# Two-layer decoder trunk: fixed order of the inner norms, two PSUM banks for the turned chunks, and a fourth kept-back unit outside the weight slots

## The chip, the core and the metric

The kernel runs on one core of a Trainium2 chip. The metric is device microseconds (us) of one execution, smaller is better. Engines are called by the profile's names: PE (TensorE, matmuls), PEld (its weight loads), DVE (VectorE), ACT (ScalarE), POOL (GpSimd) and SP (SyncE, which issues the transfers here).

## The reference, cut to what matters

Two layers over 256 tokens of width 2048. Each layer has a token mixer (layer 0 forgetting attention, "fox"; layer 1 sliding-window attention, "swa") and a gated ConvFFN. Each of these four sub-layers ends in a LayerNorm, and the next begins with a modulation by columns that come from the conditioning vector `c`:

```python
for i in range(DEPTH):
    sh1, sc1, g1, sh2, sc2, g2 = split(silu(c) @ ada_w[i] + ada_b[i], 6)
    h = x * (1 + sc1) + sh1
    y = fox_attention(h, ...) if i % 2 == 0 else swa_attention(h, ...)
    x = layer_norm(ALPHA * x + (1 + g1) * y, ln_mix_g[i], ln_mix_b[i])
    h = x * (1 + sc2) + sh2
    y = conv_ffn(h, ...)
    x = layer_norm(ALPHA * x + (1 + g2) * y, ln_ffn_g[i], ln_ffn_b[i])
```

## The kernel before, in words

**Arithmetic.** Every large product is done in split form: an operand is rounded to a "high" part (fp32r) and the rest is a "low" part, and three matmuls (high x high, high x low, low x high) are summed. Weights stream in blocks: a *unit* is two 128-row slices of the weight by 512 columns. `stream` loads it (`w`), ACT rounds it to the high part (`wh`, L252), DVE subtracts to get the low part (`wl`, L263). `wh` and `wl` come from a pool of four slots each; the raw `w` tiles come from a pool of six, which the rows of the conditioning matrix (`wa`, L395) and the LayerNorm gains (`ln`, L667) share.

**Activations.** `x` holds the 256 tokens as two halves of 128 rows each, the *first rows* (t = 0) and the *second rows* (t = 1), by four column blocks of 512 (d = 0 to 3). `hH`/`hL` is the turned (transposed), modulated input of a sub-layer, in 16 chunks of 128 columns; both lie in one tile, so the profile and the order call both `hH`.

**The joints.** Between two sub-layers the last column block of the last projection must be finished, added to `x` and normalised before the next projection can start. Three such inner *joints* exist, near 450, 1188 and 1452 us; class `Edge` writes them. To overlap, the last projection keeps its last four units back (`x_mm_end`): for these it does the first rows at once and the second rows afterwards, while the first rows go through residual, statistics and norm. The next projection's first block does the reverse (`x_mm_start`): its first four units are done for the first rows, then for the second rows. The kept units need storage beyond the four slots: `spares` puts three of them into free parts of the `hH` buffer, the fourth stays in a weight slot.

`residual_rows` is the chain of one half: product times gate (L634), add to `x` (L636), statistics (L638, L641, L643), reciprocal root on POOL (L644), the negated mean times root (L646). `normalise(d, ts, act)` scales a column block on ACT (L659) for the halves in `act`, else on DVE (L661). `turn_rows` transposes four chunks of one half on PE (L514) into one PSUM bank; `mod_rows` then makes for a pair of chunks the high parts on ACT (L522) and an fp32 copy `t` on DVE (L526) or ACT (L524), and DVE subtracts to the low part (L527). The chunks from 8 on are turned for both halves together (`mod_turn` L477, `mod_pair` L491, L495, L84, L85).

**What sets the order.** Each engine runs its own list in order. A scheduler lays out the lists at build time; an instruction under `pin` keeps its place in program order, the others may be moved. `affine` (L680, L681) multiplies the normalised `x` by the LayerNorm gains later, in the background, one instruction pair per step of the stream.

## Time and profile before

| | |
|---|---|
| median of 3 runs | 2201.17 us (2200.56 to 2203.99) |
| profiled execution | 2202.95 us, its span 2201.1 us |
| granted PE clock, mean | 0.991 |
| PE / DVE / ACT busy | 2135.2 / 1767.4 / 1175.3 us of the span |
| HBM read | 594.18 MB, 271 GB/s over the span |

A row of the groups reads: line, engine, operation, output <- inputs, shapes, count, then busy us and mean ns of one, then idle time ahead of it and what ended that. A row of the timeline reads: start, duration, engine, line, operation; in brackets the idle time before it and the engine and tile that ended it. A row of the stages gives for each engine busy us and (in brackets) instructions, then the granted PE clock, the DMA share and GB/s.

### The profile page before, as it was taken

What the parts mean: (1) busy time and instruction counts of PE and PEld (TensorE: products, weight loads), DVE (VectorE), ACT (ScalarE), POOL (GpSimd) and SP (SyncE); (2) the same over time, 40 slices, a digit from 0 to 9 for tenths busy, and PEclk for the clock granted to TensorE, in tenths of its full rate; (3) what the DMA queues carried; (4) which work ended last, traced back from release to release, by engine and by line L of the source; (5) the groups of instructions that cost most, each with busy time, mean ns of one, the idle gap of its engine ahead of it and who ended that gap; (6) DMA issues with size and microseconds to landing.
All of it is one profiled execution on the core that took longest, in us unless ns stands there. A gap on an engine that the chain in (4) does not pass through costs nothing.

```text
span 2201.1 us, 35820 instructions
## 1 busy us (share of the span) xinstructions
PE 2135.2 (97%) x14488; PEld 1935.5 (88%) x14488; DVE 1767.4 (80%) x2431; ACT 1175.3 (53%) x1821; POOL 11.5 (1%) x34
## 2 busy tenths in 40 slices
PE   6999999889999999999999999989999999999997
PEld 6999887669999888999987777769999988999986
DVE  7988899979889988898996888679788655666765
ACT  4546566356575433555554577556555633555541
POOL 1000000000000000000000000000000000000000
PEclk9999999999999999999999999999999999999999
DMA  9998999948888899888885665437777655555552
GB/s 388 417 368 309 356 342 342 340 151 328 322 293 320 329 347 361 322 330 297 323 334 208 229 262 197 170 137 287 268 268 268 211 191 191 194 193 197 195 197 97
DMA packets 89654, 598.60 MB, mean 272 GB/s; under 512 B 10016, under 2 KB 12352, under 8 KB 21136
## 3 DMA queue, kind: packets, MB, share of 16 engines
q1 hardware_dynamic: 89312, 595.87, 73.3%
q8 instruction: 113, 1.85, 0.3%
q0 software_dynamic: 176, 0.44, 0.1%
q14 instruction: 53, 0.43, 0.1%
HBM read 594.18 MB, written 2.10 MB: 271 GB/s over the span
## 4 chain that ended last, share of the span: by engine, by line
PE 79%; DVE 12%; ACT 5%; issue 2%; DMA 2%; SPq 0%; POOL 0%; POOLq 0%; DVEq 0%; ACTq 0%
PE ws L75 45%; PE xs L75 32%; DVE wl L263 4%; DVE wa L395 4%; ACT wh L252 2%; DMA w<-in_fox_w_in_dram 2%; ACT pr L712 1%; DVE pr L708 1%; PE o L75 1%; ACT hH L522 0%; DVE x L636 0%; DVE stats L638 0%; PE T L739 0%; ACT x L659 0%; PE sm L477 0%
## 5 line engine op out<-in xcount | busy, mean ns | idle before, releaser
L252 ACT CAST wh<-w 128x1024 fp32r<-128x1024 f32 x715 | 752.1, 1053 | 756.8 <-PE xs L75 346.7
L263 DVE TENSOR_TENSOR wl<-w,wh 128x1024 fp32r<-128x1024 f32 x715 | 869.1, 1221 | 331.0 <-ACT wh L252 328.4
L75 PE MATMUL ws<-hH,wh 128*128 128x256 f32 x6400 | 1097.5, 276 | 7.5 <-ACT hH L504 6.1
L75 PEld LDWEIGHTS ws<-hH,wh 128*128 128x128 f32 x6400 | 968.4, 188 | 10.9 <-ACT hH L504 6.7
L75 PE MATMUL ws<-hH,wl 128*128 128x256 f32 x3200 | 879.9, 276 | 2.4 <-DVE wl L263 2.4
L75 PEld LDWEIGHTS ws<-hH,wl 128*128 128x128 f32 x3200 | 601.0, 188 | 3.4 <-DVE wl L263 3.3
L395 DVE CUSTOM_DVE_ANT_0 wa<-wa,cb,acol 128x2048 f32<-128x2048 f32 x192 | 449.6, 2344 | 0.2 <-DVE cb L134 0.2
L75 PE MATMUL xs<-wh,gT 128*128 128x512 f32 x1352 | 417.4, 389 | 0.0
L75 PEld LDWEIGHTS xs<-wh,gT 128*128 128x128 f32 x1352 | 253.8, 188 | 52.5
L75 PE MATMUL xs<-wh,hH 128*128 128x512 f32 x816 | 276.6, 406 | 17.2 <-DVE hH L527 13.8
L75 PE MATMUL xs<-wl,gT 128*128 128x512 f32 x676 | 263.0, 389 | 0.0
L75 PEld LDWEIGHTS xs<-wh,hH 128*128 128x128 f32 x816 | 153.0, 191 | 56.2 <-DVE hH L527 17.9
L75 PE MATMUL xs<-wl,hH 128*128 128x512 f32 x408 | 163.3, 400 | 3.0 <-DVE wl L263 3.0
L75 PEld LDWEIGHTS xs<-wl,gT 128*128 128x128 f32 x676 | 126.9, 188 | 26.4
L1110 ACT ACTIVATE u<-ws,ccol 128x256 f32<-128x256 f32 x176 | 96.8, 562 | 51.8 <-PE ws L75 42.1
L75 PE MATMUL xs<-wh,oT 128*128 128x512 f32 x352 | 118.9, 407 | 0.0
L75 PEld LDWEIGHTS xs<-wl,hH 128*128 128x128 f32 x408 | 78.0, 191 | 19.3 <-DVE wl L263 3.6
L1111 DVE SCALAR_TENSOR_TENSOR u<-ws,ccol,u 128x255 f32<-128x255 f32 x176 | 82.2, 477 | 14.1 <-ACT u L1110 14.1
L1113 DVE SCALAR_TENSOR_TENSOR u<-ws,ccol,u 128x254 f32<-128x254 f32 x176 | 83.2, 477 | 2.2
L75 PEld LDWEIGHTS xs<-wh,oT 128*128 128x128 f32 x352 | 68.1, 194 | 15.6 <-ACT oT L84 0.7
L75 PE MATMUL xs<-wl,oT 128*128 128x512 f32 x176 | 71.2, 405 | 6.8 <-DVE wl L263 6.8
L712 ACT ACTIVATE pr<-pr,nm 128x128 f32<-128x128 f32 x96 | 43.2, 452 | 27.3 <-DVE nm L708 27.2
(204 smaller groups left out, 1180.9 us busy)
## 6 DMA issues: line engine op xcount, KB each, us to landing
wa<-in_ada_w_dram SPq DMA_DIRECT2D x192, 1024.0 KB, 6.8
w<-in_ffn_w_up_dram SPq DMA_DIRECT2D x176, 1024.0 KB, 5.2
w<-in_ffn_w_down_dram SPq DMA_DIRECT2D x88, 1024.0 KB, 5.1
w<-in_fox_w_in_dram SPq DMA_DIRECT2D x60, 512.0 KB, 8.3
w<-in_swa_w_in_dram SPq DMA_DIRECT2D x20, 1024.0 KB, 6.2
w<-in_fox_w_in_dram SPq DMA_DIRECT2D x18, 1024.0 KB, 7.3
w<-in_fox_w_o_dram SPq DMA_DIRECT2D x16, 1024.0 KB, 6.8
w<-in_swa_w_o_dram SPq DMA_DIRECT2D x16, 1024.0 KB, 4.8
```

What stands on the lines that cost most here:

```text
L75: return nc.tensor.matmul(o, lhsT, rhs, start=start, stop=stop, **kw)
L252: pin(nc.scalar.copy(h, w), False)
L263: pin(nc.vector.tensor_tensor(l, w, f32(h), op=ALU.subtract), behind[0] > 0)
L395: return nc.vector.tensor_tensor_reduce(w, w, cb, 1.0, acol[:, l, v * KC + k:v * KC + k + 1], ALU.mult, ALU.add, cv[:, k:k + 1])
L708: nc.vector.tensor_tensor_reduce(pr[:, b:e].rearrange("p (a k) -> p a k", k=P), S_ps[:, b:e].rearrange("p (a k) -> p a k", k=P), mk, -1.0, ...
L712: nc.scalar.activation(pr[:, b:e], pr[:, b:e], AF.Exp, bias=nm[:, r:r + 1], scale=-1.0, accum_out=ss[:, r:r + 1])
L1110: nc.scalar.activation(u, pf, AF.Identity, bias=cw(CW, f), scale=cw(2, f))
L1111: nc.vector.scalar_tensor_tensor(u[:, 1:], pf[:, :S - 1], cw(1, f), u[:, 1:], op0=ALU.mult, op1=ALU.add)
L1113: nc.vector.scalar_tensor_tensor(u[:, 2:], pf[:, :S - 2], cw(0, f), u[:, 2:], op0=ALU.mult, op1=ALU.add)
```

## The change

It has five parts.

1. `turn_rows` spreads the four turned chunks of a half over two PSUM banks, one for even and one for odd chunks. `mod_rows` makes the fp32 copy `t` first, the even chunk on ACT (L534 in the new file) and the odd one on DVE (L536; for two pairs of the first rows both on ACT), then rounds both chunks in one ACT instruction from `t` (L537), and returns the subtraction (L538) for the caller to place.
2. The inner norms are ordered by hand. For the first rows both needed blocks (d = 0, 1) are normalised on DVE (L674), the negated mean (now `centre`, L659) comes after them. For the second rows residual, statistics and norm stand before the next projection's first unit; d = 0 on DVE, d = 1 on ACT (L672). Residual and norm instructions of the joints are pinned. The later blocks d = 2 and 3 of the first rows, which ACT did at the start of the joint, are done at their program place.
3. The fourth kept unit gets storage outside the weight slots: the fourth spare in `hpad` for the ConvFFN's joint, four small tiles (`Pair`, `eh`/`el`, each half a unit) for the two attention joints. A unit in a `Pair` is rounded and subtracted in two halves.
4. `affine` of the middle joint starts 12 steps late and not 7.
5. The dead switches `alone` and `behind` go; in the last LayerNorm L646 is no longer issued.

```diff
-            h, l = spare.get(kc) or (hl.tile([P, 2, WB], F32R, tag=n, name=n) for n in ("wh", "wl"))
-            pin(nc.scalar.copy(h, w), False)
+            h, l = spare[kc]() if kc in spare else (hl.tile([P, 2, WB], F32R, tag=n, name=n) for n in ("wh", "wl"))
+            pieces = [(h, l, w)] if not isinstance(h, Pair) else [(h[:, i, :], l[:, i, :], w[:, i, :]) for i in range(2)]
+            for hp, _, wp_ in pieces:
+                pin(nc.scalar.copy(hp, wp_), False)
...
-            def residual_(w=w, h=h, l=l, go=go):
-                pin(nc.vector.tensor_tensor(l, w, f32(h), op=ALU.subtract), behind[0] > 0)
-                behind[0] -= 1
+            def residual_(pieces=pieces, go=go):
+                for hp, lp, wp_ in pieces:
+                    nc.vector.tensor_tensor(lp, wp_, f32(hp), op=ALU.subtract)
...
+    class Pair:
+        def __init__(self, name):
+            self.t = [gtile(name).rearrange("p a b -> p (a b)") for _ in range(2)]
+        def __getitem__(self, i):
+            return self.t[i[1]]
...
-        return {nk - 8 + 2 * i: (at(32 + i * 2 * WB), at(60 + (8 + 2 * i) * WB)) for i in range(3)}
+        out = {nk - 8 + 2 * i: lambda i=i: (at(32 + i * 2 * WB), at(60 + (8 + 2 * i) * WB)) for i in range(4)}
+        if held:
+            out[nk - 2] = lambda: (Pair("eh"), Pair("el"))
+        return out
...
-        o = bank()
+        os = [bank() for _ in range(2)]
         for j in range(4):
-            nc.tensor.transpose(o[:, j * P:(j + 1) * P], x[:, t, (k + j) * P:(k + j + 1) * P], ident)
-        return o
+            nc.tensor.transpose(os[j % 2][:, j // 2 * P:(j // 2 + 1) * P], x[:, t, (k + j) * P:(k + j + 1) * P], ident)
+        return os
...
-            pin(nc.scalar.activation(hH[:, k + j, r], src, AF.Identity, bias=b, scale=g))
-            if on_act:
+            if j < act:
                 pin(nc.scalar.activation(tmp[:, j, :], src, AF.Identity, bias=b, scale=g))
             else:
-                pin(nc.vector.tensor_scalar(tmp[:, j, :], src, g, b, op0=ALU.mult, op1=ALU.add), t > 0)
-        pin(nc.vector.tensor_tensor(hL[:, k:k + 2, r], tmp, f32(hH[:, k:k + 2, r]), op=ALU.subtract), t > 0)
+                pin(nc.vector.tensor_scalar(tmp[:, j, :], src, g, b, op0=ALU.mult, op1=ALU.add))
+        pin(nc.scalar.copy(hH[:, k:k + 2, r], tmp))
+        return lambda: pin(nc.vector.tensor_tensor(hL[:, k:k + 2, r], tmp, f32(hH[:, k:k + 2, r]), op=ALU.subtract))
...
                 residual_rows(ps, last, gates[self.gate], True, 0)
+                normalise(0, (0,), ())
+                normalise(1, (0,), ())
+                centre(0)
...
-            elif i == 1:
-                normalise(0, (0,), ())
-                normalise(1, (0,))
...
-            else:
+            elif i == 4:
                 residual_rows(ps, last, gates[self.gate], True, 1)
-                self.rows(0, 6, True)
+                two, three = (self.rows(0, k, act=2) for k in (4, 6))
+                two()
+                centre(1)
+                normalise(0, (1,), ())
+                three()
+                normalise(1, (1,), (1,))
...
-                later([affine(self.name, self.ll, 0 if self.v else 7)])
+                later([affine(self.name, self.ll, 0 if self.v else 12)])
```

Three places show how the lists move. First DVE at the first joint, from the first rows' residual on; `wl` rows are low parts of the next projection's units.

```order
L634 TENSOR_TENSOR t_4348<-xs_4188,gate_2670 128x512
L263 TENSOR_TENSOR wl_4436<-w_4433,wh_4435 128x1024
L636 TENSOR_TENSOR x_112<-x_112,t_4348 128x512
L638 BN_STATS stats_147<-x_112 128x6
L641 BN_AGGR mv_4352<-stats_147 128x2
L643 TENSOR_SCALAR mv_4352<-mv_4352 128x1
L646 SCALAR_TENSOR_TENSOR rs_4354<-mv_4352,rs_4354 128x1
L661 TENSOR_SCALAR x_112<-x_112,mv_4352,rs_4354 128x512
```

The same place now:

```order
L644 TENSOR_TENSOR t_4352<-xs_4188,gate_2670 128x512
L264 TENSOR_TENSOR wl_4440<-w_4437,wh_4439 128x1024
L646 TENSOR_TENSOR x_112<-x_112,t_4352 128x512
L264 TENSOR_TENSOR wl_4450<-w_4437,wh_4449 128x1024
L648 BN_STATS stats_147<-x_112 128x6
L651 BN_AGGR mv_4356<-stats_147 128x2
L653 TENSOR_SCALAR mv_4356<-mv_4356 128x1
L674 TENSOR_SCALAR x_112<-x_112,mv_4356,rs_4358 128x512 x2
L659 SCALAR_TENSOR_TENSOR rs_4358<-mv_4356,rs_4358 128x1
```

A second `wl` now stands inside the first rows' chain, both norms follow the root directly, and the negated mean comes behind them. Second, DVE at the middle joint, from the second pair of chunks of the first rows to the second rows' statistics (`t_12150`, now `t_12142`, is the second rows' residual).

```order
L527 TENSOR_TENSOR hH_146<-t_12115,hH_146 128x2x128
L526 TENSOR_SCALAR t_12127<-sm_12110,G_12091,B_12092 128x128
L263 TENSOR_TENSOR wl_12179<-w_12166,wh_12178 128x1024
L526 TENSOR_SCALAR t_12127<-sm_12110,G_12091,B_12092 128x128
L527 TENSOR_TENSOR hH_146<-t_12127,hH_146 128x2x128
L527 TENSOR_TENSOR hH_146<-t_12138,hH_146 128x2x128
L634 TENSOR_TENSOR t_12150<-xs_11891,gate_6524 128x512
L636 TENSOR_TENSOR x_112<-x_112,t_12150 128x512
L527 TENSOR_TENSOR hH_146<-t_12160,hH_146 128x2x128
L638 BN_STATS stats_147<-x_112 128x6
L641 BN_AGGR mv_12154<-stats_147 128x2
L643 TENSOR_SCALAR mv_12154<-mv_12154 128x1
```

Now:

```order
L538 TENSOR_TENSOR hH_146<-t_12131,hH_146 128x2x128
L644 TENSOR_TENSOR t_12142<-xs_11891,gate_6524 128x512
L646 TENSOR_TENSOR x_112<-x_112,t_12142 128x512
L648 BN_STATS stats_147<-x_112 128x6
L651 BN_AGGR mv_12146<-stats_147 128x2
L653 TENSOR_SCALAR mv_12146<-mv_12146 128x1
L538 TENSOR_TENSOR hH_146<-t_12151,hH_146 128x2x128
L659 SCALAR_TENSOR_TENSOR rs_12148<-mv_12146,rs_12148 128x1
L674 TENSOR_SCALAR x_112<-x_112,mv_12146,rs_12148 128x512
L538 TENSOR_TENSOR hH_146<-t_12155,hH_146 128x2x128
```

The `wl` between the first rows' chunks is gone from here (that unit is now done before the chain), and the low parts of the first rows' third and fourth pair of chunks stand behind the second rows' statistics. Third, ACT at the middle joint, at the end of the second rows; `x` rows are norms of the first rows (d = 2, then 3), `t_12250` and `t_12267` belong to chunks 8 to 11. Before:

```order
L522 ACTIVATE hH_146<-sm_12219,B_12092,G_12091 128x128
L524 ACTIVATE t_12230<-sm_12219,B_12092,G_12091 128x128
L252 CAST wh_12329<-w_12327 128x1024
L491 ACTIVATE t_12256<-sm_12250,B_12092,G_12091 128x256
L491 ACTIVATE t_12273<-sm_12267,B_12092,G_12091 128x256
L84 CAST hH_146<-t_12256 128x512
L84 CAST hH_146<-t_12273 128x512
```

Now:

```order
L534 ACTIVATE t_12231<-sm_12209,B_12092,G_12091 128x128
L252 CAST wh_12315<-w_12313 128x1024
L537 CAST hH_146<-t_12231 128x2x128
L672 ACTIVATE x_112<-x_112,rs_12085 128x512
L252 CAST wh_12318<-w_12313 128x1024
L252 CAST wh_12323<-w_12321 128x1024
L502 ACTIVATE t_12250<-sm_12244,B_12092,G_12091 128x256
L502 ACTIVATE t_12267<-sm_12261,B_12092,G_12091 128x256
L84 CAST hH_146<-t_12250 128x512
L84 CAST hH_146<-t_12267 128x512
L672 ACTIVATE x_112<-x_112,rs_12085 128x512
```

The first rows' norms of d = 2 and 3 now stand here, and two casts of later weights stand between the first of them and chunk 8. In the swa stage the list of DVE has 16 `affine` instructions, ten of which stood ahead of the rope of the first query block before and none now; in SP's list the two `ln` transfers stand behind four more (`wa`, `w`, `w`, `wa`).

## The prediction

> **What bounds the kernel now.** I read the shares of the page first, then busy time by stage, then PE's waits in the stages that are not full, then the timeline there.

> ```profile
> PE 2135.2 (97%) x14488; PEld 1935.5 (88%) x14488; DVE 1767.4 (80%) x2431; ACT 1175.3 (53%) x1821; POOL 11.5 (1%) x34
> ...
> PE 79%; DVE 12%; ACT 5%; issue 2%; DMA 2%; SPq 0%; POOL 0%; POOLq 0%; DVEq 0%; ACTq 0%
> ```

> PE is busy for 97% and carries 79% of the chain that ended last. So only a stage in which PE idles can give time back. By stage (start:end, length, then busy PE, PEld, DVE, ACT, POOL, granted clock, DMA share, GB/s):

> ```profile
> 448.00:486.00 38.00, 31.33 (x139) 23.66 (x138) 25.38 (x47) 21.08 (x41) 1.13 (x2) 0.96 0.30 102
> 496.00:735.00 239.00, 239.00 (x2099) 238.62 (x2099) 217.53 (x284) 142.89 (x217) 0.00 (x0) 1.00 0.85 316
> 735.00:866.00 131.00, 131.00 (x583) 108.56 (x582) 115.12 (x119) 53.66 (x56) 0.00 (x0) 1.00 0.93 354
> 1186.00:1216.00 30.00, 24.62 (x109) 18.57 (x108) 20.83 (x42) 18.58 (x37) 1.10 (x2) 0.94 0.20 70
> 1450.00:1480.00 30.00, 24.15 (x113) 17.84 (x112) 21.20 (x43) 18.06 (x36) 1.10 (x2) 1.00 0.21 70
> ```

> The long stages are full (239 of 239, 131 of 131; there a matmul starts every 131/583 = 0.225 us). The three inner joints are not: PE idles 6.67, 5.38 and 5.85 us, 17.9 together, and no engine is full there, so it is a chain of hand-overs. PE's waits in these joints (total, times, longest), first, middle and third joint:

> ```profile
> PE xs L75 <- DVE hH L527: 5.2, 4, 2.3
> PE sm L514 <- DVE x L661: 1.4, 2, 1.0
> ...
> PE xs L75 <- DVE hH L527: 4.3, 3, 2.3
> PE sm L514 <- DVE x L661: 1.0, 2, 0.5
> ...
> PE xs L75 <- DVE hH L527: 4.3, 3, 2.3
> PE sm L514 <- DVE x L661: 1.1, 2, 0.6
> PE xs L75 <- ACT hH L84: 0.4, 1, 0.4
> ```

> They are 6.6, 5.3 and 5.8 us: low parts of turned chunks (L527), and norms ahead of the transposes (L661). The middle joint, PE:

> ```profile
> 1190.58 0.66 PE L514 MATMUL sm<-ident,x 128*128 128x128 f32 x4 [0.54 <-DVE x L661]
> ...
> 1193.37 0.39 PE L75 MATMUL xs<-wh,gT 128*128 128x512 f32 x1
> ...
> 1197.00 0.73 PE L75 MATMUL xs<-wh,hH 128*128 128x512 f32 x2 [1.36 <-DVE hH L527]
> ...
> 1201.37 1.11 PE L514 MATMUL sm<-ident,x 128*128 128x128 f32 x8 [0.43 <-DVE x L661]
> ...
> 1204.42 0.50 PE L75 MATMUL xs<-wh,hH 128*128 128x512 f32 x1 [0.68 <-DVE hH L527]
> ...
> 1209.88 0.73 PE L75 MATMUL xs<-wh,hH 128*128 128x512 f32 x2 [2.27 <-DVE hH L527]
> ```

> 0.54 + 1.36 + 0.43 + 0.68 + 2.27 = 5.28 us. And what made them, on DVE, ACT and POOL:

> ```profile
> 1189.33 0.55 POOL L644 TENSOR_TENSOR rs<-mv,mhalf 128x1 f32<-128x1 f32 x1 [722.70 <-DVE mv L643]
> 1189.98 0.54 DVE L661 TENSOR_SCALAR x<-x,mv,rs 128x512 f32<-128x512 f32 x1
> 1191.53 0.44 ACT L522 ACTIVATE hH<-sm,B,G 128x128 fp32r<-128x128 f32 x1
> 1193.06 0.41 DVE L526 TENSOR_SCALAR t<-sm,G,B 128x128 f32<-128x128 f32 x1 [0.64 <-ACT hH L522]
> 1193.50 0.42 DVE L527 TENSOR_TENSOR hH<-t,hH 128x256 fp32r<-128x256 f32 x1
> 1194.94 1.23 DVE L263 TENSOR_TENSOR wl<-w,wh 128x1024 fp32r<-128x1024 f32 x1 [0.53 <-ACT wh L252]
> 1197.20 0.68 DVE L634 TENSOR_TENSOR t<-xs,gate 128x512 f32<-128x512 f32 x1
> 1200.11 0.55 POOL L644 TENSOR_TENSOR rs<-mv,mhalf 128x1 f32<-128x1 f32 x1 [10.24 <-DVE mv L643]
> 1202.06 0.46 ACT L522 ACTIVATE hH<-sm,B,G 128x128 fp32r<-128x128 f32 x1 [4.00 <-PE sm L514]
> ```

> In one bank ACT and DVE take turns: 1191.53 to 1193.92, 2.4 us for a pair of chunks. The fourth unit's `wl` (1.23) stands between the pairs, since its slot was the kept unit's, and the second rows' chain starts at 1197.20 although PE's last product for it began at 1193.4.

> **The change part by part, middle joint.** Three more prices:

> ```profile
> L84 ACT CAST gT<-u 128x256 fp32r<-128x256 f32 x88 | 35.2, 403 | 13.5 <-DVE u L1147 12.5
> L491 ACT ACTIVATE t<-sm,B,G 128x256 f32<-128x256 f32 x12 | 6.1, 559 | 3.8 <-PE sm L477 3.8
> L659 ACT ACTIVATE x<-x,rs 128x512 f32<-128x512 f32 x9 | 7.0, 806 | 25.1 <-DVE rs L646 25.1
> ```

> *First norm.* It no longer stands behind L646 on DVE; that one was 0.07 us ahead. The wait of 0.54 becomes 0.46.

> *Two banks.* The new chain of a pair, from the start of its transposes: 0.69 until ACT may read (1201.37 to 1202.06), 0.46 for `t` on ACT with DVE's 0.41 beside it, 0.40 for the rounding of both chunks (the 128x256 cast above), 0.42 for the subtraction (as L527), and about 0.05 at each hand-over: 2.1 us. ACT is free for it, since the norms of d = 1 to 3 of the first rows (0.8 each) no longer stand ahead. From transposes at 1190.50 the first pair is ready at 1192.6 and the second, one ACT and one DVE round later, at 1193.9. PE wants the second pair at about 1194.9. The wait of 1.36 goes.

> *Second rows first.* L634's successor may start at 1193.93, when DVE has done the second pair. The chain took 1197.20 to 1200.11 until POOL, 2.9 us with one low part of 0.3 in it; now 2.6, to 1196.55. POOL (0.55) is done at 1197.15, the norm of d = 0 (0.54) at 1197.8. This is a wait added to DVE: queued behind it are the low parts of the third and fourth pair. The third's now comes at about 1197.0, where PE wants it at 1196.7, less the 0.16 by which a matmul's record outlasts its issue: a new wait of 0.2. The second rows' transposes then find their norm done when PE comes to them, at 1198.0: the 0.43 goes. Their chunks have 2.1 us each and PE has a unit of 12 or 6 matmuls before each: 0.68 and 2.27 go.

> *What is late next.* ACT now does the norms of d = 2 and 3 of the first rows (0.81 each) behind the second rows' chunks, and two casts of later weights (1.05 each) ahead of chunk 8. Laid out with those durations, PE comes to chunk 8's transposes 0.1 before their norm is done; comes to unit 5 at 1207.4 while chunk 8's high part (0.56 + 0.56 + 0.6 behind the casts) is ready at 1208.55, a wait of 1.0; and waits 0.25 for the norm of d = 3. New waits: 1.35.

> Middle joint: 5.3 goes to 0.46 + 0.2 + 1.35 = 2.0, a gain of 3.3. The third joint has the same rows and 0.4 more, which the new order does not have: 5.8 to 2.1, 3.7.

> *First joint.* There the low part of a next unit stands inside the first rows' chain, because its place is behind the residual although DVE idled 5 us before it; now there are two.

> ```profile
> 450.93 0.69 DVE L634 TENSOR_TENSOR t<-xs,gate 128x512 f32<-128x512 f32 x1 [5.05 <-PE xs L75]
> 451.54 1.22 DVE L263 TENSOR_TENSOR wl<-w,wh 128x1024 fp32r<-128x1024 f32 x1
> ```

> The chain gets 1.13 later (1.22, pipelined). PE meanwhile does all of the kept unit's products, so the first transposes wait 0.55 at 457.0; the first pair costs 0.4, and the third pair, behind the second rows' chain, 1.45; then 1.3 as above. 6.6 goes to 3.7, a gain of 2.9.

> *The kept unit in half tiles*: 2 x 0.62 for one 1.05 on ACT and 2 x 0.69 for 1.22 on DVE, +0.3, in the 5.05 us that DVE idles. Without that cover it would cost 0.3 twice. Priced at 0.

> *Fewer stops and the clock.* Each of some six stops a joint slows the matmul behind it by 0.1 (the two at 1197.00 take 0.73, so start 0.34 apart where 0.225 is usual); about half go: 0.5 in all. After the longest stop the granted clock fell in two of the joints:

> ```profile
> 470.00:481.00 11.00, 8.36 (x32) 6.40 (x33) 8.29 (x14) 9.11 (x18) 0.00 (x0) 0.84 0.28 95
> 1204.00:1215.00 11.00, 8.31 (x32) 6.41 (x33) 8.15 (x14) 9.12 (x18) 0.00 (x0) 0.84 0.26 95
> 1468.00:1479.00 11.00, 7.86 (x36) 5.84 (x37) 8.58 (x15) 9.54 (x18) 0.00 (x0) 1.00 0.28 95
> ```

> 0.16 x 11 = 1.8 us in each of two. With shorter stops this may go (3.5) or stay (0): nothing shows which. I take 1.5, nearer to staying, since PE still stops eight times.

> [...] The rows differ: 0.84 twice behind such a stop, and 1.00 behind the same stop in the third joint.

> *The later `affine`.* Ten of 16 instructions, 0.69 us each, move from ahead of the first query block's rope to behind it.

> ```profile
> 1239.29 0.69 DVE L680 SCALAR_TENSOR_TENSOR x<-x,ln 128x512 f32<-128x512 f32 x1
> ...
> 1230.00:1260.00 30.00, 29.58 (x145) 23.78 (x144) 29.37 (x47) 15.17 (x22) 0.00 (x0) 1.00 0.75 268
> 1260.00:1290.00 30.00, 29.16 (x170) 22.93 (x169) 28.72 (x80) 21.89 (x55) 0.00 (x0) 1.00 0.80 316
> ```

> DVE is full in both stages, yet PE idles only 0.42 and 0.84. Bounds: -1.3 (that idle goes) and +6.9 (all ten land on PE). Nearest is the first stage: DVE with ten of them and nothing to spare cost PE 0.42. I take 0; freed DVE time before the rope lets the low parts run ahead. SP's two `ln` transfers are moved past four others, and the weights behind keep their place in its list: 0, bounds ±0.5.

> *The end.* L646, 0.16 twice, off the last chain: -0.1.

> Sum: -3.3 - 3.7 - 2.9 - 0.5 - 1.5 - 0.1 = -12.0. These durations are of the profiled execution, 2202.95 (span 2201.1 and 1.85 around it), 1.8 above the median of the runs. Against that median I take 0.5 off for waits that such a layout misses: 2201.2 - 11.5 = 2189.7.

> **Rivals.** Within 0.2% (4.4 us; about what a measurement here can tell from no change) counts as the same.

> 1. *The waits move on.* PE waits again for chunks 8 to 11, whose norms and casts now stand late on ACT. For: 1.35 of new wait is already in the layout. Against: ACT is busy 18.6 of 30 there. If each joint loses 3 more, the gain is 12.0 - 9.0 = 3: 2198.
> 2. *The swa stage turns DVE-bound, slower.* DVE is at 28.72 of 30 behind the rope; each moved instruction may delay a `wl` and, by the pair's softmax in the same list, transposes that PE meets in order. All 16 landing twice: 2 x 16 x 0.69 = 22.1 less 12.0 is 10.1 more: 2211. It decides from 16.4 more idle PE in 1230 to 1400. Against: DVE was as full before and PE lost 0.42.
> 3. *More than forecast.* The clock stays up (2 more) and chunk 8 is in time (3 more): 2185.
> 4. *The order does not do what it says*: the first joint gains nothing from its second `wl` and the clock stays as it is: 12.0 - 2.9 - 1.5 = 7.6, 2193.6, still faster.

> **How the numbers follow.** Forecast (2187 to 2192.5) 0.50; the fourth 0.20; the third 0.15; the first 0.11; the second 0.04. So faster 0.85, same 0.11, slower 0.04. The range reaches from the third case to the better half of the first: 2184.5 to 2197.5; it leaves out the second, most of the first and the far side of the third, below 0.2.

> **What would show it.** Right: PE's waits in the three joints fall from 17.7 to about 8; no wait over 1.5; chunk pairs take about 2.1 us from transposes to low part; the first joint's first transposes wait no less than before; DVE's second-rows residual starts within 0.3 us of the second pair's low part; PE's idle in the swa stage stays under 3 us. Wrong: waits of 2 us for chunk 8 or the third pair, or PE idle behind `wl` after the rope.

## The result and the profile after

The changed kernel takes 2184.87 us (median of 4 runs, 2183.98 to 2185.87), the kernel before 2202.58 in the same comparison (4 runs, 2200.56 to 2204.05): a ratio of 0.992, interval 0.9903 to 0.9938. The forecast was 2189.7. So it is faster, and by more than the likeliest case: 2184.87 lies 0.4 inside the lower end of the range, where the third rival put it (2185). The profiled execution after took 2185.40, its span is 2183.6.

The page after, shares and chain:

```profile
PE 2129.5 (98%) x14488; PEld 1932.3 (88%) x14488; DVE 1763.2 (81%) x2425; ACT 1169.7 (54%) x1805; POOL 11.8 (1%) x34
...
PE 82%; DVE 10%; ACT 5%; issue 1%; DMA 1%; SPq 0%; POOL 0%; DVEq 0%; ACTq 0%; POOLq 0%
```

PE's share of the chain went from 79% to 82%, and its busy time from 2135.2 to 2129.5 although the number of matmuls is the same: 0.5 of this is of the start-up, and in the joints the matmuls that ran at half clock do so no more. By stage after, the three joints and the swa stage (start:end, length, busy PE, PEld, DVE, ACT, POOL, granted clock, DMA share, GB/s):

```profile
448.00:480.00 32.00, 29.19 (x138) 22.00 (x137) 24.23 (x45) 18.05 (x34) 1.24 (x2) 1.00 0.31 108
1180.00:1206.00 26.00, 24.76 (x121) 18.87 (x120) 20.43 (x41) 16.27 (x32) 1.22 (x2) 1.00 0.18 63
1438.00:1466.00 28.00, 26.65 (x129) 20.41 (x128) 21.75 (x44) 17.69 (x34) 1.14 (x2) 1.00 0.20 67
1220.00:1390.00 170.00, 166.49 (x955) 128.61 (x955) 139.18 (x368) 116.00 (x285) 0.00 (x0) 1.00 0.62 224
```

PE idles 2.81, 1.24 and 1.35 us in the joints, 5.4 together, where it was 17.9; the granted clock is 1.00 in all three, where it was 0.96, 0.94 and 1.00. PE's waits in them, first, middle and third joint (total, times, longest):

```profile
PE xs L75 <- DVE hH L538: 1.1, 1, 1.1
PE xs L75 <- ACT hH L84: 0.7, 1, 0.7
PE xs L75 <- ACT hH L537: 0.5, 1, 0.5
PE sm L525 <- DVE x L674: 0.4, 1, 0.4
...
PE xs L75 <- ACT hH L84: 0.7, 1, 0.7
PE sm L525 <- DVE x L674: 0.5, 1, 0.5
...
PE xs L75 <- ACT hH L84: 0.7, 1, 0.7
PE sm L525 <- DVE x L674: 0.6, 1, 0.6
```

Eight waits are left of 17, and the waits for low parts (`hH` from DVE) are gone but for one. The middle joint on PE, DVE, ACT and POOL, as before the change:

```profile
1184.25 0.66 PE L525 MATMUL sm<-ident,x 128*128 128x128 f32 x4 [0.47 <-DVE x L674]
...
1185.88 0.43 DVE L538 TENSOR_TENSOR hH<-t,hH 128x256 fp32r<-128x256 f32 x1 [0.53 <-ACT hH L537]
...
1187.16 0.42 DVE L538 TENSOR_TENSOR hH<-t,hH 128x256 fp32r<-128x256 f32 x1 [0.53 <-ACT hH L537]
...
1187.50 0.69 DVE L644 TENSOR_TENSOR t<-xs,gate 128x512 f32<-128x512 f32 x1
...
1190.05 0.42 DVE L538 TENSOR_TENSOR hH<-t,hH 128x256 fp32r<-128x256 f32 x1
1190.21 0.66 POOL L654 TENSOR_TENSOR rs<-mv,mhalf 128x1 f32<-128x1 f32 x1 [6.60 <-DVE mv L653]
...
1190.51 0.30 PEld L75 LDWEIGHTS xs<-wh,hH 128*128 128x128 f32 x2 [0.32 <-DVE hH L538]
...
1191.58 0.66 PE L525 MATMUL sm<-ident,x 128*128 128x128 f32 x4
```

The second rows' residual (L644) starts when the second pair's low part ends, and POOL gets the second rows 7.15 us after the first (1183.06 to 1190.21; before 10.78). The third pair's low part (1190.05) comes just when PE wants it, and the second rows' transposes (1191.58) start with no wait.

Where the time came from can be read by matching. PE issues the same 14,488 matmuls in nearly the same order, so I compared the start of the matmul of the same number in two traces. The differences, in us against the kernel before, by stretch of its trace:

```
                  to 449   joint 1  joint 2   swa    joint 3   end    sum from 449
after              -0.54    -5.72    -6.19   +0.79    -5.28   -0.60     -17.0
```

Between these stretches the changed kernel neither gains nor loses (0.01 at most). The 0.54 ahead of the first joint is of the start-up, which the change leaves alone; it moved between -2.4 and +0.3 in the profiles below. So I compare the kernels from 449 on, and give the timed ratios beside it. Each kernel has one trace, of one execution; where that one lies far from the median, the text says so.

### The profile page after: what moved, and what is told of

Its sections match the earlier page's. It is cut to its first block, busy times and chain, and to the rows that moved or that the text cites. A ratio compares the mean times of both kernels' runs of the same rounds, so it can differ in the third digit from the quotient of the medians.

```text
span 2183.6 us, 35813 instructions
## 1 busy us (share of the span) xinstructions
PE 2129.5 (98%) x14488; PEld 1932.3 (88%) x14488; DVE 1763.2 (81%) x2425; ACT 1169.7 (54%) x1805; POOL 11.8 (1%) x34
## 3 DMA queue, kind: packets, MB, share of 16 engines
q8 instruction: 113, 1.85, 0.3%
## 4 chain that ended last, share of the span: by engine, by line
PE 82%; DVE 10%; ACT 5%; issue 1%; DMA 1%; SPq 0%; POOL 0%; DVEq 0%; ACTq 0%; POOLq 0%
PE ws L75 46%; PE xs L75 34%; DVE wa L406 3%; DVE wl L264 3%; ACT wh L252 2%; DMA w<-in_fox_w_in_dram 1%; ACT pr L725 1%; DVE pr L721 1%; PE o L75 0%; DVE x L646 0%; ACT pr L1088 0%; DVE stats L648 0%; PE T L752 0%; PE sm L75 0%; PE sm L488 0%
## 5 line engine op out<-in xcount | busy, mean ns | idle before, releaser
L252 ACT CAST wh<-w 128x1024 fp32r<-128x1024 f32 x712 | 749.1, 1055 | 748.0 <-PE xs L75 336.5
L75 PE MATMUL ws<-hH,wh 128*128 128x256 f32 x6400 | 1098.0, 276 | 8.0 <-ACT hH L515 7.2
L75 PEld LDWEIGHTS ws<-hH,wh 128*128 128x128 f32 x6400 | 968.3, 188 | 11.4 <-ACT hH L515 7.6
L75 PE MATMUL ws<-hH,wl 128*128 128x256 f32 x3200 | 879.9, 276 | 2.4 <-DVE wl L264 2.4
L75 PEld LDWEIGHTS ws<-hH,wl 128*128 128x128 f32 x3200 | 601.3, 188 | 3.4 <-DVE wl L264 3.4
L75 PE MATMUL xs<-wh,gT 128*128 128x512 f32 x1344 | 414.7, 389 | 0.0
L75 PEld LDWEIGHTS xs<-wh,gT 128*128 128x128 f32 x1344 | 252.3, 188 | 52.1
L75 PE MATMUL xs<-wh,hH 128*128 128x512 f32 x800 | 269.4, 402 | 6.2 <-ACT wh L252 2.4
L75 PE MATMUL xs<-wl,gT 128*128 128x512 f32 x672 | 261.4, 389 | 0.0
L75 PEld LDWEIGHTS xs<-wh,hH 128*128 128x128 f32 x800 | 149.3, 189 | 41.8 <-ACT hH L84 3.5
L75 PE MATMUL xs<-wl,hH 128*128 128x512 f32 x400 | 158.4, 396 | 3.3 <-DVE wl L264 3.3
L75 PEld LDWEIGHTS xs<-wl,gT 128*128 128x128 f32 x672 | 126.1, 188 | 26.3
L75 PE MATMUL xs<-wh,oT 128*128 128x512 f32 x352 | 119.1, 407 | 0.2 <-ACT oT L84 0.2
L75 PEld LDWEIGHTS xs<-wl,hH 128*128 128x128 f32 x400 | 75.6, 189 | 18.6 <-DVE wl L264 3.9
L75 PEld LDWEIGHTS xs<-wh,oT 128*128 128x128 f32 x352 | 68.2, 194 | 15.6 <-ACT oT L84 0.7
L75 PE MATMUL xs<-wl,oT 128*128 128x512 f32 x176 | 71.2, 405 | 6.8 <-DVE wl L264 6.8
```

What stands on the lines that cost most here:

```text
L75: return nc.tensor.matmul(o, lhsT, rhs, start=start, stop=stop, **kw)
L252: pin(nc.scalar.copy(hp, wp_), False)
```

## The experiments

Each is timed against the kernel before on the same chip; runs of the changed kernel are in the first comparison (0.992). Stretches by the same matching:

```
                  joint 1  joint 2   swa    joint 3   end    sum from 449   timed ratio (interval)
one bank           -3.31    -3.80   +0.68    -3.12   -0.59     -10.1     0.9959 (0.9946 to 0.9971)
slot unit          -5.12    -4.91   +0.65    -4.28   -0.62     -14.3     0.9937 (0.9924 to 0.9949)
late second rows   +0.56    -2.51   +0.67    -1.81   -0.60      -3.7     0.9983 (0.9974 to 0.9992)
affine at 7        -5.74    -6.18   -0.01    -5.29   -0.59     -17.8     0.9920 (0.9906 to 0.9933)
wl first           -6.38    -6.21   +0.73    -5.29   -0.60     -17.8     0.9920 (0.9907 to 0.9934)
PE order           -7.75    -6.19   +0.75    -5.27   -0.62     -19.1     0.9913 (0.9900 to 0.9927)
norm on DVE        -4.98    -5.45   +0.59    -4.52   -0.61     -15.0     0.9936 (0.9924 to 0.9949)
stop               -1.94    -1.15   +0.76    -2.59   -0.60      -5.5     0.9974 (0.9964 to 0.9983)
early norm         -6.81    -7.27   +0.57    -6.39   -0.59     -20.5     0.9901 (0.9886 to 0.9916)
together           -8.82    -7.25    0.00    -6.34   -0.61     -23.0     0.9895 (0.9882 to 0.9909)
before + banks     -3.09    -2.96   +0.22    -0.59   -0.01      -6.4     0.9976 (0.9966 to 0.9985)
```

My theory was that the joints are one chain of hand-overs, so each part of the change that shortens a link gives its length; the rivals were that one part alone carries the gain, or that the clock does. The first four undo one part each. Not undone alone are the new order of the first rows' norms and the later place of their norms of d = 2 and 3; the run with the late norms on DVE bears on the second.

**One bank.**

```diff
-        os = [bank() for _ in range(2)]
+        os = (lambda o: [o[:, :2 * P], o[:, 2 * P:]])(bank())
```

> The changed kernel with the four turned chunks of a half in one PSUM bank again (t first and the one rounding stay, and the order of the joints stays). Theory (the hand-overs of the chunk pairs are part of the chain): in one bank ACT's and DVE's reads for t take turns, so each of the first two pairs of a joint takes 0.4 us longer, and the second rows' residual, which stands behind the second pair, starts 0.4 to 0.8 later: 1.2 to 2.4 us for three joints, about 1.8, so 2186.7. Rival (the bank does not matter, only the order does): 0 within 0.3, 2184.9.

Measured 2192.88 us, 8 slower than the changed kernel and not 1.8. The mechanism is there. The first pair of the middle joint on ACT and DVE, in one bank:

```profile
1187.52 0.66 PE L525 MATMUL sm<-ident,x 128*128 128x128 f32 x4 [0.46 <-DVE x L674]
...
1188.21 0.46 ACT L534 ACTIVATE t<-sm,B,G 128x128 f32<-128x128 f32 x1 [9.11 <-PE sm L525]
...
1188.71 0.41 DVE L536 TENSOR_SCALAR t<-sm,G,B 128x128 f32<-128x128 f32 x1 [0.72 <-ACT t L534]
...
1189.59 0.43 DVE L538 TENSOR_TENSOR hH<-t,hH 128x256 fp32r<-128x256 f32 x1 [0.47 <-ACT hH L537]
```

and in two:

```profile
1184.83 0.46 ACT L534 ACTIVATE t<-sm,B,G 128x128 f32<-128x128 f32 x1 [9.00 <-PE sm L525]
1184.94 0.41 DVE L536 TENSOR_SCALAR t<-sm,G,B 128x128 f32<-128x128 f32 x1 [0.23 <-PE sm L525]
```

In one bank DVE's read waits for ACT's (it starts 0.50 behind it, and names ACT as its releaser); in two it starts 0.11 behind it. From the transposes to the start of the low part it is 2.07 against 1.63, the 0.4 that I expected. Why they take turns no run shows; in the one-bank rows the two reads don't overlap (ACT's ends at 1188.67, DVE's starts at 1188.71). What I had wrong was the size. ACT's gaps of 0.48 while it waits for DVE are filled in the built list with casts of later weights (1.04 each), and one now stands between chunk 8's `t` and its rounding:

```profile
1204.60 1.02 ACT L502 ACTIVATE t<-sm,B,G 128x256 f32<-128x256 f32 x2 [0.39 <-PE sm L488]
...
1205.51 1.04 ACT L252 CAST wh<-w 128x1024 fp32r<-128x1024 f32 x1
...
1206.44 1.15 ACT L84 CAST hH<-t 128x512 fp32r<-128x512 f32 x2
...
1207.12 0.50 PE L75 MATMUL xs<-wh,hH 128*128 128x512 f32 x1 [1.77 <-ACT hH L84]
```

PE waits 1.77 for chunk 8 in place of 0.7, in all three joints: 3.2 of the 6.9 that this kernel loses from 449 on. Of the other 3.7, 2.7 are longer waits for the pairs, and PE stops 13 times in the joints and not 8.

**The fourth unit in a weight slot.**

```diff
-        out = {nk - 8 + 2 * i: lambda i=i: (at(32 + i * 2 * WB), at(60 + (8 + 2 * i) * WB)) for i in range(4)}
-        if held:
+        out = {nk - 8 + 2 * i: lambda i=i: (at(32 + i * 2 * WB), at(60 + (8 + 2 * i) * WB)) for i in range(3)}
+        if False:
```

> The changed kernel with the fourth kept unit in a weight slot again, in all three joints; the rest stays. Theory (what stands inside the chain costs what it takes): one rounding (1.05 on ACT) and one wl (1.22 on DVE) come back between the first rows' second pair and the second rows' statistics; third pair and second rows' norm come 1.1 to 2 us later where PE has 0 to 1 to spare: 1.5 a joint, +4.5, and a joint whose stop gets over 2 us may lose 1.7 more to the clock: 2188 to 2193, about 2190. Rival (the unit's place is only storage; the fixed order is what counts): less than 1 slower, 2185 to 2186.

Measured 2188.12, 3.3 slower (2.7 in the trace), at the low edge of what the theory gave and above the rival: 0.6, 1.3 and 1.0 in the three joints. The waits for L538 grow from 1.1 to 1.8 in the first joint and from nothing to 0.9 and 0.8 in the others; no stop gets over 1.2 and the clock stays up.

**The second rows' chain late.**

```diff
-                residual_rows(ps, last, gates[self.gate], True, 1)
                 two, three = (self.rows(0, k, act=2) for k in (4, 6))
                 two()
+                three()
+                residual_rows(ps, last, gates[self.gate], True, 1)
                 centre(1)
                 normalise(0, (1,), ())
-                three()
```

> The changed kernel with the second rows' residual, statistics and norm behind the low parts of the third and fourth pair of chunks, as before the change, all still pinned. Theory (the second rows' chain sets the end of the joint): residual starts 2.3 us later, at the middle joint 1189.8 and not 1187.5, so PE waits 2 to 3.4 us ahead of the second rows' transposes and the third pair's wait of the first joint (1.1) is gone: +2.2 a joint, 6.6 together; each stop of over 2 us may take 1.7 more of clock: 2191.5 to 2196.5, about 2193. Rival (PE has enough first-row work to cover the later chain): within 2, 2183 to 2187.

Measured 2198.60, 13.7 slower: more than the theory's upper end, and nowhere near the rival. The residual starts 2.3 late, as expected, behind all four low parts of the first rows. That is a little more than an undoing: in the kernel before, the fourth low part stood behind the addition, so about 0.4 of each joint is this run's own. The middle joint:

```profile
1194.33 0.43 DVE L538 TENSOR_TENSOR hH<-t,hH 128x256 fp32r<-128x256 f32 x1 [0.53 <-ACT hH L537]
1195.48 0.42 DVE L538 TENSOR_TENSOR hH<-t,hH 128x256 fp32r<-128x256 f32 x1 [0.72 <-ACT hH L537]
1196.63 0.43 DVE L538 TENSOR_TENSOR hH<-t,hH 128x256 fp32r<-128x256 f32 x1 [0.72 <-ACT hH L537]
1196.97 0.68 DVE L644 TENSOR_TENSOR t<-xs,gate 128x512 f32<-128x512 f32 x1
```

Beside that, chunk 8 waits 1.8 in each joint as in one bank (3.3 together), and the clock was halved twice in the first joint, which lost 2.7 more than each of the other two. The trace is of the slowest of 11 executions, 1.0 above the median. Of the parts undone alone this one costs most. Its share of the gain can't be read off, though: the four parts undone alone add up to 22.1, more than the 17.0 of the whole change, so they overlap.

**The affine at 7 steps.** The edit is `0 if self.v else 7`.

> The changed kernel with the affine of the middle joint 7 steps late and not 12. Theory A (as predicted, no net effect): 0 within 0.4. Theory B (the moved affine instructions are what PE now waits for behind the rope, 3.5 us of idle PE in the swa stage against 2.3 before): 1.2 faster, about 2183.7. Rival C (the later affine helps the wl ahead of the rope and so a part of the gain is its own): 1 to 3 slower.

Measured 2183.92, and the ratio is the changed kernel's (0.9920), so the times don't decide it. The traces do: the swa stage gains 0.80 by this edit alone and nothing else moves. That is theory B with 0.8 in place of 1.2. PE's waits there, the changed kernel:

```profile
PE S L75 <- DVE qL L85: 2.1, 2, 1.2
PE qp L1052 <- DVE qb L1007: 1.3, 2, 0.8
```

and with the affine at 7:

```profile
PE S L75 <- DVE qL L85: 1.7, 2, 0.8
PE qp L1052 <- DVE qb L1007: 0.4, 1, 0.4
```

Behind the rope DVE was full already (28.72 of 30 us before the change, in 1260 to 1290); the moved instructions make PE wait for the turned queries (`qb`).

The next four ask what still bounds the joints, and what the clock did.

**Two `wl` ahead of the first joint's chain.**

```diff
-            if n > 2 - (items[0] not in weights):
+            if n > (4 if items[0] in final else 2) - (items[0] not in weights):
...
-            settle(2)
+            settle(4 if work[0] in final else 2)
```

> The changed kernel with the two wl that stand inside the first rows' chain of the first joint moved ahead of it, into the 5.07 us in which DVE idles there; no other instruction moves on any engine. Theory (PE's list now sets the first joint's beginning): the chain is ready 2.2 us earlier, but PE's list has the first transposes behind all of the kept units' products, which PE ends at 455.9; so only the wait of 0.42 ahead of them goes, and the pairs start 0.4 earlier: 0.4 faster, 2184.5. Rival (the chain sets it): 2.2 faster, 2182.7.

Measured 2184.12; the first joint gains 0.65 in the trace (0.4 expected, 2.2 by the rival), and the wait of 0.4 for the norm is gone while the other three stay. So the two `wl` cost 0.65 together, though in my layout the second alone made the chain 1.13 later: for most of that time PE still had products of its own to do.

**And PE's order fixed.** In addition the first rows' two groups of transposes are placed ahead of the fourth kept unit's products, both pinned:

```diff
...
-            elif i == 2:
+            elif i == 3:
                 place(60 if self.v else 32)
                 self.turn(0, 0)
                 self.rows(0, 0)()
-            elif i == 3:
                 self.turn(0, 4)
                 self.rows(0, 2)()
```

> As the kernel before in this list (two wl ahead of the first joint's chain), and besides, in each joint PE's list has the first rows' transposes (both groups) fixed ahead of the fourth kept unit's second-row products, not behind them (first joint) or split around half a unit (the other two). Theory: in the first joint transposes run at 454.4 and not 456.3, the 6 products cover the first pair, and the second rows' residual starts 2 us earlier, so the waits 0.42, 0.54 and 1.08 go: 2.0 faster there. In the other two the first transposes come 0.7 later in the list: their wait of 0.47 to 0.56 goes but the pairs come 0.2 later: between 0.3 faster and 0.2 slower each. Sum 2183 to 2182.5. Rival (other waits take the place of those three at once): within 0.5 of the kernel before in this list.

Measured 2182.59. The first joint gains 2.0 against the changed kernel, as worked out, and the other two nothing (0.00 and 0.01): their wait for the norm goes and one of the same length for the third pair comes. Its waits, first joint, then middle:

```profile
PE xs L75 <- ACT hH L84: 0.7, 1, 0.7
PE xs L75 <- DVE hH L538: 0.5, 1, 0.5
...
PE xs L75 <- ACT hH L84: 0.8, 1, 0.8
PE xs L75 <- DVE hH L538: 0.6, 1, 0.6
```

**The late norms on DVE.** `normalise(2, act=())` and `normalise(3, act=())`.

> The changed kernel with the first rows' norms of d = 2 and 3 on DVE (0.54 each) and not on ACT (0.82 each). Theory (chunk 8 waits because its high part stands behind a norm and two casts on ACT): ACT reaches chunk 8 about 0.8 us earlier in each joint and PE's wait of 0.73 for its high part goes: 0.7 a joint, 2.1 faster, 2182.8. Rival (DVE has no room: its wl stand between the same chunks): the norm comes later on DVE than it did on ACT, or a wl does, and PE waits as long: within 0.5 of 2184.9.

My theory falls: 2188.18, 3.3 slower, and worse than the rival (the trace, 2.0 slower, is of the fastest of five executions). Chunk 8 waits 1.8 in each joint. Its last transposes are done no earlier, because the norm of the second rows still stands behind a `wl` on DVE and now behind another norm; and a cast stands between `t` and the rounding again:

```profile
1196.10 1.23 DVE L264 TENSOR_TENSOR wl<-w,wh 128x1024 fp32r<-128x1024 f32 x1 [0.55 <-ACT wh L252]
...
1197.58 1.00 DVE L674 TENSOR_SCALAR x<-x,mv,rs 128x512 f32<-128x512 f32 x2
...
1199.03 1.02 ACT L502 ACTIVATE t<-sm,B,G 128x256 f32<-128x256 f32 x2 [0.71 <-PE sm L488]
...
1199.95 1.04 ACT L252 CAST wh<-w 128x1024 fp32r<-128x1024 f32 x1
...
1200.88 1.14 ACT L84 CAST hH<-t 128x512 fp32r<-128x512 f32 x2
```

ACT, one norm shorter, sat idle for 0.71 until the transposes came (the row at 1199.03): freeing ACT alone doesn't bring chunk 8 forward, since DVE's norm holds its transposes.

**One stop in each joint.** Four additions into a scratch tile ahead of the third low part:

```diff
+                z = ttile(); [pin(nc.vector.tensor_tensor(z, x[:, 0, :512], x[:, 0, 512:1024], op=ALU.add)) for _ in range(4)]
                 two, three = (self.rows(0, k, act=2) for k in (4, 6))
```

> The changed kernel with four idle additions of DVE (0.69 each, into a scratch tile that nothing reads) ahead of the third pair's low part in each joint, which makes one stop of PE of 2.7 us there (3.8 in the first joint); nothing else moves in the joints. In the runs so far the halved clock comes in stretches of 3.413 us whose starts lie on a grid of that step, each behind a stretch of that grid in which PE was busy for less than 0.47. Theory (busy share of a fixed stretch): the stop itself costs 2.7 a joint, 8.2 together; the clock is halved behind those stops alone of which 1.8 us or more fall in one stretch of the grid, two joints of three in the mean, 1.7 us each: 2193 to 2198. [...] Rival B (the number of stops matters, not their length): the clock stays as it is, 2193.

Measured 2196.52, within the theory's numbers. PE stops once for 3.9, 2.7 and 2.6 us. The stages behind these stops:

```profile
462.00:473.00 11.00, 7.33 (x29) 5.97 (x30) 7.01 (x18) 4.51 (x9) 0.93 (x1) 0.84 0.00 0
...
1197.00:1208.00 11.00, 10.62 (x41) 8.68 (x41) 5.72 (x14) 6.55 (x12) 0.00 (x0) 0.70 0.00 1
...
1460.00:1471.00 11.00, 10.03 (x50) 7.71 (x50) 8.00 (x18) 8.11 (x15) 0.00 (x0) 1.00 0.01 1
```

The clock fell in the first two joints and not in the third, though its stop is as long as the second's. The third joint lost 2.7 against the changed kernel, the stop alone; the middle one 5.0, with two stretches at half clock. So the length of a stop alone does not decide: half clock followed a stop of 2.7 here and not one of 2.6, and in the kernel before, whose longest stops are 2.3, it followed two of the three. Rival B would have kept all three joints at full clock. What tells the stops apart in the traces is where they lie in the grid: in the traces before and after, each change of the granted clock lies a whole number of steps of 3.413 us from the first one. PE's busy share of a grid stretch of 3.413 us in the joints (start, share), and the clock granted in the stretch behind it:

```
before             473.2  0.34 half    1207.1  0.34 half    1469.9  0.52 full
late second rows   463.3  0.41 half     477.0  0.47 half
stop               462.9  0.18 half    1193.3  0.41 half    1459.6  0.59 full
one bank           473.6  0.48 full    1204.0  0.48 full
norm on DVE       1198.3  0.48 full    1457.7  0.48 full
after              lowest 0.70, all full
```

Shares up to 0.47 were followed by half clock, shares from 0.48 on were not. Over all steps of the traces before and after that began at full clock, the start-up included, the highest share followed by half clock is 0.41 and the lowest followed by full clock 0.52: no step of the two falls out of this order. Steps that ran at half clock went otherwise: in these two traces, those with a share up to 0.67 were followed by another at half clock, and those from 0.93 on by full clock; so some stretches last two steps. The second step in the middle joint above stood behind a share of 0.81.

**The second rows' norm early.**

```diff
-                normalise(1, (1,), (1,))
+                normalise(1, (1,), (1,)); normalise(2, (1,), ())
...
-                normalise(2)
+                normalise(2, (0,))
```

> The changed kernel with the second rows' norm of d = 2 on DVE right behind the first rows' fourth low part and the norm of d = 1, in a gap of 0.42 that DVE has there, and not behind a wl seven instructions later. Theory (chunk 8 waits for that norm: its second transposes start at 1199.14, 0.05 behind the norm, and ACT reads them at 1199.84): the transposes of chunks 8 and 9 go in one piece, one cast of a later weight stands ahead of ACT's reading and not two, and the high part is ready 0.7 earlier: PE's wait of 0.73 goes in each joint, 2.1 faster, 2182.8. Rival (DVE has no room for 0.54 in a gap of 0.42): the second rows' first pair comes later and PE waits there: within 0.5 of 2184.9.

Measured 2180.67, 4.2 faster than the changed kernel (twice the 2.1 expected; 3.5 in the trace). Chunk 8's wait is gone in all three joints:

```profile
1191.49 0.54 DVE L674 TENSOR_SCALAR x<-x,mv,rs 128x512 f32<-128x512 f32 x1
...
1197.83 1.09 PE L488 MATMUL sm<-ident,x 128*128 128x128 f32 x8
...
1198.62 1.01 ACT L502 ACTIVATE t<-sm,B,G 128x256 f32<-128x256 f32 x2
...
1199.53 1.13 ACT L84 CAST hH<-t 128x512 fp32r<-128x512 f32 x2
```

Each joint gains 1.1 for a wait of 0.73: one stop costs more than the idle row says. Part of this is that the list also moved: one cast of a later weight, not two, now stands ahead of ACT's reading. Before chunk 8 in the changed kernel the distance from one matmul's start to the next is 1.13 in place of 0.228, which is 0.90, and the transposes in one piece save one change-over: in the changed kernel the record of the product behind four transposes is 0.48 long, that of the next one 0.40 (at 1198.52 and 1198.84).

**The three edits together** (PE's order with the `wl`, the affine at 7, the early norm).

> The changed kernel with three edits together: the two wl ahead of the first joint's chain with PE's fixed order (alone 2.3 faster), the affine of the middle joint at 7 (alone 0.8 faster in the swa stage of the profile), and the early norm of the run before in this list (2.1 by its theory). Theory (different waits, so they add): 5.2 faster, 2179.7. Rival (a wait that goes lets the next one show, as in the two kernels in which chunk 8 waited 1.8): the early norm brings nothing beside the others: 2181.8.

Measured 2179.70 (2177.58 to 2180.04), the number of the theory: ratio 0.9895 (0.9882 to 0.9909) to the kernel before, the fastest of all. From 449 on it gains 6.0 over the changed kernel; its only waits in the joints are 0.5, 0.6 and 0.5 for the third pair.

**The kernel before with the banks alone.** `turn_rows` and `mod_rows` as changed, the calls and their order as before.

> The kernel before with one part of the change alone: two PSUM banks for the turned chunks, t first, one rounding for both chunks; the order of the joints, the unit in a slot and the affine as before. Theory (the turn-taking lengthens each pair by 0.4, and the chain behind it, whatever the order): 0.8 to 1.5 a joint, and the clock stays up where the longest stop of 2.27 gets under 1.8: 3 to 6 faster, about 2198. Rival (with the old order the second rows' chain is late anyway, and shorter pairs wait for it): less than 1 faster, 2201 to 2202.

Measured 2197.43, 5.5 faster (2198 expected). In its trace (mean clock 0.995, the changed kernel's 0.994) the clock doesn't fall in the joints any more, which is about 2.9 of the 6.4 from 449 on (worked out in the next section). But this trace is of the fastest of nine executions, which went from 2194.41 to 2199.49; the start-up differs by 2.7 at most between the traces here, and what else made the others longer is not shown. The changed kernel less its banks keeps 10.1 of 17.0, and the banks alone give 6.4. That looks like a sum, but each of the three has the 2.9 of the clock once; without it 7.2 and 3.5 stand against 14.1. Of the 3.4 between them, 3.2 is the cast ahead of chunk 8 in one bank. So the banks are worth about 3.5 in either order, and one bank costs 3.2 more in the new order because its list puts that cast where PE waits for it.

## Why the prediction was right, and where its sizes were off

The sign and the mechanism held: the gain lies in the three joints (17.2 from 449 on; with 0.8 lost in the swa stage and 0.6 gained at the end it is 17.0), each undone link gives time back, and no single part carries it all. The sum was -11.5 where the two profiles differ by 17.55, of which 0.54 is the start-up. That the time is the third rival's number is in part luck: of its two conditions the clock came true, while chunk 8 still waits 0.7 in each joint, and shorter waits elsewhere and dearer stops made up for it.

One figure of the prediction doesn't come out of its own terms: half of six stops in three joints at 0.1 each is 0.9, not 0.5.

- *Waits, -9.9 (3.3 + 3.7 + 2.9).* Measured -12.5 (17.9 to 5.4). In the middle and third joint I had 0.2 for the third pair, 1.0 for chunk 8's high part and 0.25 for the norm of d = 3; measured 0, 0.7 and 0. In the first joint 0.55, 0.4, 1.45 and 1.3 became 0.4, 0.5, 1.1 and 0.7. Chunk 8 was late not by ACT's casts alone, as I had it, but by DVE's norm behind a `wl` as well: in the changed kernel this norm ends at 1199.09 in the middle joint, its transposes follow at 1199.14, and ACT's reading starts at 1199.84, just as its two casts are done. Moving the norm took the wait away, and one of the two casts with it; how much is each one's was not taken apart.
- *Clock, -1.5, and fewer stops, -0.5.* Together -4.7, what is left of the joints (17.2 - 12.5), and no run measures them apart. The third joint lost no clock in either trace: it gained 5.28, of which 4.50 are waits, so the four stops that went are worth about 0.2 each. By that price the first and the middle joint (1.86 and 2.05 left, two and three stops gone) leave 1.5 each for the clock: an estimate of -2.9 for the clock, near its upper bound (two stretches of 3.413 at half clock, 3.4), and -1.8 for nine stops. The number of stops was as forecast; each costs twice the 0.1 that I read from the matmul behind it.
- *Why the clock.* I had no reason for 0.84 in two joints and 1.00 in the third behind the same stop. What differs in the trace is the place of the stop in the grid: the step with the stop has a share of 0.34, 0.34 and 0.52. If I slide a stretch of 3.413 over the traces, the lowest share in a joint is 0.34 in the kernel before, in each of the three, and it is below 0.47 for some 60% of the positions; in the changed kernel it is never below 0.68. So by the table two joints of three was the luck of one execution's grid, and the changed kernel stays above every share there that half clock followed, wherever the grid lies.
- *The affine, 0 (bounds -1.3 and +6.9).* Measured +0.8: matched by number, 1.05 is gained by 1260 of the trace before and 1.8 lost from 1270 to 1290. PE's idle in the swa stage is 3.5, over the 3 that I allowed. The rival of a DVE-bound stage was right in direction there and far from deciding.
- *The end, -0.1.* Measured -0.6. L646 waited for POOL, and an instruction of 0.75 that needs nothing from POOL (L1209) stood behind it on DVE. The end of the kernel before, POOL and DVE:

```profile
2191.69 0.93 POOL L644 TENSOR_TENSOR rs<-mv,mhalf 128x1 f32<-128x1 f32 x1 [9.95 <-DVE mv L643]
2192.65 0.16 DVE L646 SCALAR_TENSOR_TENSOR rs<-mv,rs 128x1 f32<-128x1 f32 x1 [0.44 <-POOL rs L644]
2192.73 0.75 DVE L1209 SCALAR_TENSOR_TENSOR x<-x,mv,ln 128x512 f32<-128x512 f32 x1
```

Now both of the L1209 (L1222 in the new file, 2174.51 to 2175.91) run beside POOL (2174.74 to 2175.66). The kernel with the banks alone, which still issues L646, has -0.01 at the end.

- *The half tiles, SP: 0.* Nothing in the traces speaks against it, and no run takes either alone.

Of the signs given beforehand: waits fall to 5.2 and not 8; none over 1.5 (the longest is 1.1); a chunk pair takes 2.06 from transposes to the end of its low part (2.1); the first joint's first transposes wait 0.42, and 0.41 before; the second rows' residual starts within 0.3 of the second pair's low part. One sign failed: PE's idle in the swa stage did not stay under 3. The first joint gained 3.9 of idle time with its later chain, so the fourth rival fell.

## What to carry to other kernels

Where one engine is full but for a few short joints, lay each joint out as one chain, and place what nobody waits for (casts of later weights, low parts, norms of later blocks) with the same care as the chain: here a cast of 1.04 us that came to stand ahead of chunk 8's rounding cost PE 1.1 in each joint, in three kernels. Undo a change part by part in the trace of matched matmuls before believing a story about it; 0.7 us could be read there where the runs' times could not tell it. An instruction's price is what waits behind it in its list, not its duration.
